# The down projection of a feed-forward stage: seven block products in place of eight, with the sums kept in DRAM

## The chip, the cores and the metric

The kernel runs on one core of a Trainium2 chip. The metric is the device time of one execution in microseconds. The engines are PE (TensorE, matrix products), DVE (VectorE), ACT (ScalarE), POOL (GpSimd) and SP (SyncE, which only issues transfers here). Each engine works through its own list of instructions in order, and instructions of different engines wait for each other by semaphores. PE writes into eight PSUM banks of 128 x 512 float32; the other engines read these.

## The reference, cut to what matters

One transformer block on 512 tokens of width 2048. The change touches its last part alone, the gated feed-forward of width 5632:

```
h = rms_norm(x, pre_ffn_norm)
u = causal_dwconv(h @ w_up, conv_w, conv_b)          # 512 x 11264
gate, up = jnp.split(u, 2, axis=-1)
y = (jax.nn.gelu(gate, approximate=True) * up) @ w_down    # (512 x 5632) @ (5632 x 2048)
x = x + rms_norm(y, post_ffn_norm)
```

## The kernel before, in words

All matrix products are in float32 precision made of two parts: a tile `a` is split into `hi` (rounded by an ACT copy) and `lo = a - hi` (a DVE subtraction; `split`, L132 to L134), and a product is three matmuls, hi·hi + hi·lo + lo·hi. So each weight tile that comes from DRAM costs one ACT and one DVE instruction per 128 x 512 piece before PE can use it.

Work is a list of *units*: a unit is a weight tile of 128 x 1024 (512 KB) and the matmuls that use it. The main loop (L1028 on) runs unit i on PE and, between its matmuls, writes into the program the fetch of unit i+2 and the two halves of the split of unit i+1 (`prepare`), the evacuation of the unit before, and, paced by `tick`, single steps of background work. The order of every engine's list is fixed by this when the program is written; nothing is reordered on the chip.

The feed-forward has 44 column blocks j of 128 (so 88 for gate and up), in 11 groups of four. The up projection of one half of a j is two units of 24 matmuls. The background work of a j (`up_items`) is the convolution's taps (one ACT, two DVE instructions), the polynomial and tanh of the gelu, the gate and the product `prod`, whose result, the activation of 128 x 512 (features x tokens), is split into `gact[j]` = hi, lo. The down projection of group G is written after the first j of group G+1 (`down(G - 1)`): four blocks of 512 output columns g, two units each, 24 matmuls per unit, so 192 matmuls of 512 columns in a row. PE adds over the group in four banks, and `accumulate` (L865 to L870) adds each finished bank to the tile y[t, g] in SBUF by one DVE instruction. The last group is done apart, after the list, from weights kept in `H`.

SBUF has a pool of 37 tiles of 128 x 512 (`slot`), and weights have 3 buffers `raw`, 2 each of `hi` and `lo`, and 4 of `pt`, which serve as a second pair of hi and lo for units with the tag "pt".

Of the kernel before, what the change touches and what calls it, by code (L numbers as in the profile page):

```python
# [34 lines left out]
GROUP = 4  # L35
# [15 lines left out]
def body(ctx, tc, xT, x, gpre, vecs, lam4, tab, onehot, cmpm, wst, wdv, wvs, wvg, w1, w2, wo, wu, wd,  # L51
# [42 lines left out]
    park = dp.tile([PARK, 128, 512], F, name="park")  # L94
    xpark = dp.tile([S, D], F, name="xpark")

    pending = deque()
# [44 lines left out]
    def unit(src, n, mms, prep=None, after=None, start=None):  # L142
        units.append(dict(src=src, n=n, mms=mms, prep=prep, after=after, start=start, late=False, defer=False, tag=None, each=None))

# [669 lines left out]
    conv = {}  # L814
    gact = {}
    y = {}
    ysum = st.tile([128, NT, 4], F, name="ysum")

    def up_items(j, which, b):
# [24 lines left out]
        def prod():  # L844
            c = conv.pop((j, 1))
            V.scalar_tensor_tensor(c, conv.pop((j, 0)), 0.5, c, op0=OP.mult, op1=OP.mult)  # L846
            gact[j] = [slot(R), slot(R)]
            split(gact[j][0], gact[j][1], c)
        return [taps, poly, tanh, gate] if which == 0 else [taps, nothing, nothing, prod]

# [5 lines left out]
    def down_mms(b, hi, lo, G, k, t, first, last):  # L856
        ts = slice(t * 128, (t + 1) * 128)
        for c in range(2):
            gh, gl = gact[G * GROUP + 2 * k + c]
# [12 lines left out]
    NP = GROUP // 2  # L872

    def down(G):
        for g in range(4):
            box = {}
            for k in range(NP):
                def mms(hi, lo, g=g, k=k, box=box):
                    if k == 0:
                        box["b"] = [bank() for _ in range(NT)]  # L880
                    for t in range(NT):
                        down_mms(box["b"][t], hi, lo, G, k, t, k == 0, k == NP - 1)
                        yield
                        if k == NP - 1:
                            accumulate(t, g, box["b"][t], G)
                unit(wd[(G * NP + k) * 4 + g], 1024, mms)

# [77 lines left out]
    raws, his = {}, {}  # L965

    def fetch(i):
        u = units[i]
        r = raws[i] = wp.tile([128, 1024], F, name="raw", tag="raw", bufs=3)
        if i == 0:  # L970
            for c in range(2):
                load_x(c, 1)
                nc.sync.dma_start(r[:, c * 512:(c + 1) * 512], u["src"][:, c * 512:(c + 1) * 512])
            return
        if i < 8:
            load_x(2 * i, 2)
        nc.sync.dma_start(r[:, :u["n"]], u["src"])

    def prepare(i, part):
        u = units[i]  # L980
        n = u["n"]
        if u["prep"]:
            u["prep"](part)
        if part == 0:
            if u["tag"]:
# [5 lines left out]
        o = slice(part * 512, min(n, part * 512 + 512))  # L991
        split(hi[:, o], lo[:, o], raws[i][:, o])
        if part == 1:
            del raws[i]

# [3 lines left out]
    def hold_fetch(m):  # L999
        k, g = divmod(m, 4)  # L1000
        hraw[m] = wp.tile([128, 1024], F, name="raw", tag="raw", bufs=3)
        nc.sync.dma_start(hraw[m], wd[(G * NP + k) * 4 + g])

# [14 lines left out]
    deferred = []  # L1018
    for i in range(N):
        if i + 2 < N:  # L1020
            fetch(i + 2)
# [5 lines left out]
        hi, lo = his.pop(i)  # L1027
        todo = [0, 1] if i + 1 < N else []  # L1028

        def ahead():  # L1030
            if todo:
                prepare(i + 1, todo.pop(0))
            if not todo:
                while deferred:
                    deferred.pop(0)()
        for n, _ in enumerate(u["mms"](hi, lo)):
            if not u["late"]:
                ahead()
            if u["each"]:
                u["each"](n)  # L1040
            tick()
        if u["late"]:
# [27 lines left out]
    def last_sum(t, g):  # L1070
        accumulate(t, g, last[t, g], G)
        j = slot()
# [69 lines left out]
def _layout(i):  # L1142
# [19 lines left out]
    wu = f("w_up").reshape(2, 8, 128, 2, NJ, 128).transpose(4, 3, 0, 2, 1, 5).reshape(NJ * 4, 128, 1024)  # L1162
    wd = f("w_down").reshape(NJ // 2, 2, 128, 4, 512).transpose(0, 3, 2, 1, 4).reshape(NJ * 2, 128, 1024)
    vecs = np.concatenate([col(f("diff_subln")), f("cmp_pos_k").T, f("cmp_pos_v").T,
# [21 lines left out]
```

## Time and profile before

| | us |
|---|---|
| median of 3 runs | 2335.55 (2333.77 to 2335.76) |
| the profiled execution, own time | 2335.62 |
| its span, first to last instruction | 2333.5 |
| PE busy | 2307.7 (99%) |
| DVE busy | 1289.6 (55%) |
| ACT busy | 892.6 (38%) |
| POOL busy | 90.1 (4%) |

Busy is the time with at least one instruction in the engine; what matters is which engine the others wait for. The program moved 276.09 MB by DMA, 118 GB/s on the mean. The trace numbers times from the first instruction; the feed-forward runs from about 900 us to the end.

### The profile page before, as it was taken

The page shows a single profiled execution, that of the slowest core. Times are in us where ns is not written, and L with a number is a line of the kernel's source. Part 1 is how long each engine was busy: PE and PEld are TensorE (multiplying, and loading weights), DVE is VectorE, ACT ScalarE, POOL GpSimd, SP SyncE. Part 2 cuts the span into 40 slices and gives each one's busy share as a digit, 9 for nine tenths or more (in the row PEclk, how much of TensorE's full clock was granted, in tenths as well). Part 3 has the DMA queues.
Part 4 walks back from the last instruction along what each step waited for, and adds up shares of the span by engine and source line. Part 5 has one row for each costly group of instructions (what it writes and reads, how often), then busy time and mean ns, then how long its engine had stood idle before and what let it go on. Part 6 is the DMA issues. An engine that isn't in the chain of part 4 may idle for free.

```text
span 2333.5 us, 28580 instructions
## 1 busy us (share of the span) xinstructions
PE 2307.7 (99%) x10956; PEld 1917.4 (82%) x10956; DVE 1289.6 (55%) x2454; ACT 892.6 (38%) x1823; POOL 90.1 (4%) x145
## 2 busy tenths in 40 slices
PE   9999999999999999999999999999999999999997
PEld 7878888988887779788888888888888888888886
DVE  5366665657786664644545454554545454544557
ACT  6245553444465553423233232323232332323233
POOL 1001100000011101000000000000000000000002
PEclk9999999999999999999999999999999999999999
DMA  8433333432246572222222222222332222323325
GB/s 307 159 97 102 95 96 120 150 115 64 64 163 225 200 244 99 91 100 100 95 97 98 100 95 96 100 100 90 100 100 93 97 99 92 104 94 100 115 94 189
DMA packets 81689, 276.09 MB, mean 118 GB/s; under 512 B 9914, under 2 KB 9914, under 8 KB 81552
## 3 DMA queue, kind: packets, MB, share of 16 engines
q1 hardware_dynamic: 72000, 243.51, 31.6%
q0 software_dynamic: 9552, 30.76, 4.1%
q8 instruction: 86, 1.41, 0.3%
q14 instruction: 51, 0.42, 0.1%
HBM read 260.29 MB, written 17.08 MB: 119 GB/s over the span
## 4 chain that ended last, share of the span: by engine, by line
PE 92%; DVE 3%; DMA 3%; issue 1%; ACT 1%; SPq 0%; POOL 0%; DVEq 0%; ACTq 0%; POOLq 0%
PE b L73 90%; DMA raw<-wo 2%; PE b L353 1%; DVE lo L134 1%; DMA s<-xpark 1%; ACT hi L133 0%; DMA raw<-wdv 0%; DVE s L1090 0%; DMA raw<-wd 0%; DVE H L134 0%; DVE pt L134 0%; PE b L759 0%; DVE H L764 0%; DVE s L752 0%; PE b L457 0%
## 5 line engine op out<-in xcount | busy, mean ns | idle before, releaser
L73 PE MATMUL b<-H,hi 128*128 128x512 f32 (+1 forms) x3776 | 1167.2, 391 | 0.0
L134 DVE TENSOR_TENSOR lo<-raw,hi 128x512 fp32r<-128x512 f32 (+1 forms) x808 | 534.6, 686 | 741.0 <-ACT hi L133 739.9
L133 ACT ACTIVATE hi<-raw 128x512 fp32r<-128x512 f32 (+1 forms) x808 | 472.3, 621 | 895.4 <-PE b L73 747.9
L73 PEld LDWEIGHTS b<-H,hi 128*128 128x128 f32 x3776 | 697.0, 188 | 142.8 <-issue 3.5
L73 PE MATMUL b<-H,lo 128*128 128x512 f32 (+1 forms) x1888 | 733.1, 388 | 0.1
L73 PEld LDWEIGHTS b<-H,lo 128*128 128x128 f32 x1888 | 354.4, 188 | 75.2 <-DVE lo L134 1.6
L73 PE MATMUL b<-hi,s 128*128 128x512 f32 x1280 | 395.6, 389 | 0.0
L73 PE MATMUL b<-hi,H 128*128 128x512 f32 (+2 forms) x1024 | 295.4, 367 | 4.8 <-ACT hi L133 4.8
L73 PEld LDWEIGHTS b<-hi,s 128*128 128x128 f32 x1280 | 240.2, 188 | 49.8
L73 PE MATMUL b<-lo,s 128*128 128x512 f32 x640 | 249.0, 389 | 0.0
L73 PEld LDWEIGHTS b<-hi,H 128*128 128x128 f32 x1024 | 185.2, 188 | 37.7 <-ACT hi L133 8.7
L73 PE MATMUL b<-lo,H 128*128 128x512 f32 (+2 forms) x512 | 188.5, 368 | 4.1 <-DVE lo L134 3.5
L73 PEld LDWEIGHTS b<-lo,s 128*128 128x128 f32 x640 | 120.1, 188 | 25.0
L870 DVE TENSOR_TENSOR s<-s,b 128x512 f32<-128x512 f32 x160 | 107.5, 685 | 43.4 <-PE b L73 41.5
L73 PEld LDWEIGHTS b<-lo,H 128*128 128x128 f32 x512 | 96.3, 188 | 24.3 <-DVE lo L134 10.6
L338 ACT ACTIVATE s<-s,st 128x512 f32<-128x512 f32 (+3 forms) x128 | 71.0, 556 | 105.4 <-DVE st L336 105.4
L133 ACT ACTIVATE s<-s 128x512 fp32r<-128x512 f32 (+1 forms) x72 | 42.0, 583 | 117.4 <-DVE s L846 63.3
L73 PEld LDWEIGHTS b<-pt,s 128*128 128x128 f32 (+1 forms) x480 | 69.3, 166 | 5.7
L73 PE MATMUL b<-pt,s 128*62 128x256 f32 (+3 forms) x480 | 73.5, 302 | 0.0
L336 DVE CUSTOM_DVE_ANT_0 s<-b,bt 128x512 f32<-128x512 f32 (+3 forms) x128 | 57.6, 487 | 27.4 <-PE b L73 27.0
L134 DVE TENSOR_TENSOR s<-s 128x512 fp32r<-128x512 f32 (+1 forms) x72 | 45.5, 632 | 46.8 <-ACT s L133 46.8
L827 DVE SCALAR_TENSOR_TENSOR s<-b,vec,s 128x510 f32<-128x510 f32 x88 | 65.9, 749 | 3.1
(185 smaller groups left out, 1446.1 us busy)
## 6 DMA issues: line engine op xcount, KB each, us to landing
raw<-wu SPq DMA_DIRECT2D x176, 512.0 KB, 3.3
raw<-wd SPq DMA_DIRECT2D x88, 512.0 KB, 3.3
raw<-wst SPq DMA_DIRECT2D x64, 512.0 KB, 3.6
raw<-wo SPq DMA_DIRECT2D x64, 512.0 KB, 3.6
raw<-w SPq DMA_DIRECT2D x16, 512.0 KB, 4.2
raw<-wdv SPq DMA_DIRECT2D x15, 512.0 KB, 7.1
rows_b<-rv POOLq DMA_DIRECT2D x1, 5120.0 KB, 24.8
s<-xT SPq DMA_DIRECT2D x16, 256.0 KB, 6.4
```

The costliest lines, as they stand in the source:

```text
L73: T.matmul(o, a, b, start=start, stop=stop, skip_group_check=True)
L133: A.activation(hi, src, AF.Copy)
L134: V.tensor_tensor(lo, src, hi.bitcast(F), OP.subtract)
L336: V.tensor_tensor_reduce(out=z[:, :n], in0=b[:, :n], in1=bt[:, 384 - 128 * i:384 - 128 * i + n], scale=-1.0, scalar=3e38, op0=OP.add, op1= ...
L338: A.activation(z[:, :n], z[:, :n], AF.Exp, bias=m[:, j:j + 1], scale=-1.0, accum_out=s[:, j:j + 1])
L353: T.transpose(b[:, j * 128:(j + 1) * 128], z[:, j * 128:(j + 1) * 128], ident)
L827: V.scalar_tensor_tensor(c[:, 2:], b[:, :510], w[0], c[:, 2:], op0=OP.mult, op1=OP.add)
L870: V.tensor_tensor(y[t, g], y[t, g], b, OP.add)
```

## The change: what it does

For ten of the eleven groups the product (512 tokens x 512 features) x (512 features x 2048 columns) is cut once in two by two by two blocks: token halves (256), feature halves (two j each), and column halves. With A of blocks 11, 12, 21, 22 (token half, feature half) and weights likewise, eight block products become seven (the Winograd form of Strassen's identity): the left factors are 11, 12, 22 and s1 to s4, sums and differences of blocks of A; the right factors are three plain weight blocks and, for s1, s2, s3 and 22, differences of weight blocks. The function `down(G, q)` writes the seven for one pair q of 512-column blocks; it is called after the first j of the next group (q = 0) and after the second (q = 1).

- A block product is one unit of 12 matmuls of 512 columns (two feature blocks p, two token blocks t of 128, three matmuls each).
- The right factors are made on DVE just before they are split: `less` subtracts two tiles of 128 x 512 (L933), `split` then makes hi on ACT and lo on DVE. This is done per half p.
- The weights of a `q` come as one tile of 512 KB (a) and three as pairs of 256 KB in slots (b, c, d), fetched four units ahead. The main loop may now prepare unit i+2 beside unit i+1; the units have alternating tags (hi/lo and pt).
- The left factors are made in `up_items`: `sums12` and `sums34` are new steps on DVE (four half-width instructions and two splits more per pair of j).
- The products run in three chains of PSUM banks, x, y and z, in the order x y x y x z x. A chain goes on adding in its two banks after each product, and after each product both banks are copied out (ACT, or DVE for one of the two banks of every second product, L967 and L969) into slots, and a POOL DMA writes the slot to one of 16 DRAM tiles `yacc`, or adds it there (`accum_op`, L972).
- `accumulate` is gone; 16 DMAs load y back from DRAM at the last unit (`load_y`).

The diff, cut:

```
-    def tick():
-        pace["ticks"] += 1
-        pace["credit"] += pace["rate"]
+    def tick(weight=1.0):
+        pace["ticks"] += weight
+        pace["credit"] += pace["rate"] * weight
...
+            graw[j] = c
+            if j % 2 == 0:
+                t = slot(R)
+                split(t[:, LH], t[:, RH], c[:, LH])
+                fac[j // 2] = {"11": (t[:, LH], t[:, RH])}
+            else:
+                twin(j // 2, "12", "22", c)
...
+        def sums12():
+            a, b = graw[j - 1], graw[j]
+            c = graw[j, 1] = slot()
+            V.tensor_tensor(c[:, LH], a[:, RH], b[:, RH], OP.add)
+            V.tensor_tensor(c[:, RH], c[:, LH], a[:, LH], OP.subtract)
+            twin(j // 2, "s1", "s2", c)
...
-    def accumulate(t, g, b, G):
-        if G == 0:
-            y[t, g] = slot()
-            V.tensor_copy(y[t, g], b)
-        else:
-            V.tensor_tensor(y[t, g], y[t, g], b, OP.add)
...
+        def less(a, b, dst):
+            def f(p):
+                V.tensor_tensor(at(dst, p), at(a, p), at(b, p), OP.subtract)
+                return at(dst, p)
+            return f
+
+        prods = [("11", "x", (0, 0), plain("a"), [whole("a", 0, 0), halves("b", 0, 1)]),
+                 ("s1", "y", (1, 1), less("b", "a", "a"), [halves("c", 1, 1)]),
+                 ("s2", "x", (0, 1), less("c", "a", "a"), [halves("d", 1, 0)]),
+                 ("s4", "y", (0, 1), plain("c"), []),
+                 ("s3", "x", (1, 1), less("c", "b", "b"), []),
+                 ("12", "z", (0, 0), plain("d"), []),
+                 ("22", "x", (1, 0), less("d", "a", "a"), [])]
...
+            def after(n=n, ch=ch, th=th, ph=ph):
+                for t in range(2):
+                    v = slot()
+                    if t and n % 2:
+                        V.tensor_copy(v, chain[ch][t])
+                    else:
+                        A.activation(v, chain[ch][t], AF.Copy)
+                    key = 2 * th + t, 2 * ph + q
+                    if key in begun:
+                        nc.gpsimd.dma_start(yacc[key], v, accum_op=OP.add)
+                    else:
+                        begun.add(key)
+                        nc.gpsimd.dma_start(yacc[key], v)
+            unit(None, 1024, mms, after=after)
+            units[-1].update(get=lambda gets=gets: [f() for f in gets], raw=raw, defer=True, weight=0.5,
+                             tag="pt" if n % 2 else None)
...
-            if G and j == G * GROUP:
-                down(G - 1)
+            if G and j - G * GROUP < 2:
+                down(G - 1, j - G * GROUP)
+
+    units[-1]["start"] = load_y
...
-        todo = [0, 1] if i + 1 < N else []
+        todo = [(i + 1, part) for part in range(done.get(i + 1, 0), 2)] if i + 1 < N else []
+        if i + 2 < N and units[i + 2]["raw"] and not units[i]["tag"] == units[i + 1]["tag"] == units[i + 2]["tag"]:
+            todo += [(i + 2, part) for part in range(done.get(i + 2, 0), 2)]
```

How the lists stand now. First ACT, in the middle of the feed-forward, q = 0 of a group. `hi_` and `pt_` tiles are hi parts of right factors, `raw_` and other `s_` inputs are weights, `b_` are PSUM banks; L830 is the taps, L134 a hi copy, L969 a bank copied out (b_13515 and b_13516 are chain x, b_13541 is chain y).

```order
1090 L134 ACTIVATE pt_13501<-raw_13334 128x512 x2
1091 L134 ACTIVATE hi_13520<-raw_13334 128x512 x2
1092 L830 ACTIVATE s_13534<-b_13436,vec_75 128x512
1093 L134 ACTIVATE pt_13546<-s_13377 128x512
1094 L134 ACTIVATE pt_13546<-s_13378 128x512
1095 L969 ACTIVATE s_13555<-b_13515 128x512
1096 L969 ACTIVATE s_13558<-b_13516 128x512
1097 L134 ACTIVATE hi_13570<-s_13336 128x512
1098 L134 ACTIVATE hi_13570<-s_13337 128x512
1099 L969 ACTIVATE s_13581<-b_13541 128x512
```

The copies out of a bank are new on ACT, and each stands behind the hi copies of the products after next: bank x of product 11 (1095) behind the hi copies of s2 (1091) and s4 (1093, 1094), bank y of s1 (1099) behind those of s3 (1097, 1098).

The same place on DVE: L933 is a difference of weights, L135 a lo part, L831 and L832 the taps.

```order
1772 L933 TENSOR_TENSOR raw_13334<-s_13336,raw_13334 128x512
1773 L135 TENSOR_TENSOR pt_13502<-raw_13334,pt_13501 128x512
1774 L933 TENSOR_TENSOR raw_13334<-s_13337,raw_13334 128x512
1775 L135 TENSOR_TENSOR pt_13502<-raw_13334,pt_13501 128x512
1776 L933 TENSOR_TENSOR raw_13334<-s_13377,raw_13334 128x512
1777 L135 TENSOR_TENSOR lo_13521<-raw_13334,hi_13520 128x512
1778 L933 TENSOR_TENSOR raw_13334<-s_13378,raw_13334 128x512
1779 L135 TENSOR_TENSOR lo_13521<-raw_13334,hi_13520 128x512
1780 L831 SCALAR_TENSOR_TENSOR s_13534<-b_13436,vec_75,s_13534 128x511
1781 L832 SCALAR_TENSOR_TENSOR s_13534<-b_13436,vec_75,s_13534 128x510
1782 L135 TENSOR_TENSOR pt_13547<-s_13377,pt_13546 128x512
1783 L135 TENSOR_TENSOR pt_13547<-s_13378,pt_13546 128x512
```

Every difference is followed at once by the lo part of the same half, which needs ACT's hi copy in between. Before, DVE's list at the start of a down projection held lo parts, taps and the sums of L870, and no differences:

```order
1722 L134 TENSOR_TENSOR lo_13848<-raw_13802,hi_13847 128x512 x2
1723 L826 SCALAR_TENSOR_TENSOR s_13859<-b_13762,vec_75,s_13859 128x511
1724 L827 SCALAR_TENSOR_TENSOR s_13859<-b_13762,vec_75,s_13859 128x510
1725 L134 TENSOR_TENSOR lo_13884<-raw_13835,hi_13883 128x512
1726 L846 SCALAR_TENSOR_TENSOR s_13859<-s_13781,s_13859 128x512
1727 L134 TENSOR_TENSOR s_13889<-s_13859,s_13888 128x512
1728 L870 TENSOR_TENSOR s_9456<-s_9456,b_13837 128x512
1729 L134 TENSOR_TENSOR lo_13884<-raw_13835,hi_13883 128x512
1730 L870 TENSOR_TENSOR s_9466<-s_9466,b_13838 128x512
```

Second, ACT in q = 1 of the same group, around the copies of chain x after s2 (1134, 1135), for which the matmuls of s3 wait:

```order
1130 L134 ACTIVATE s_13932<-s_13878 128x512
1131 L134 ACTIVATE s_13945<-s_13942 128x512
1132 L134 ACTIVATE pt_13952<-s_13776 128x512
1133 L134 ACTIVATE pt_13952<-s_13777 128x512
1134 L969 ACTIVATE s_13961<-b_13859 128x512
1135 L969 ACTIVATE s_13964<-b_13860 128x512
1136 L134 ACTIVATE s_13970<-s_13967 128x512
1137 L134 ACTIVATE hi_13983<-raw_13695 128x512 x2
```

Here the hi parts of the activation (1130) and of s1 and s2 (1131, from `sums12`) have come ahead of the copies; in q = 0 one half-width hi part stands at this place.

## Rows read from the trace of the kernel before

**Rows 1.** The page: busy time by engine.
```profile
PE 2307.7 (99%) x10956; PEld 1917.4 (82%) x10956; DVE 1289.6 (55%) x2454; ACT 892.6 (38%) x1823; POOL 90.1 (4%) x145
```
**Rows 2.** The page: the chain that ended last, shares by engine.
```profile
PE 92%; DVE 3%; DMA 3%; issue 1%; ACT 1%; SPq 0%; POOL 0%; DVEq 0%; ACTq 0%; POOLq 0%
```
**Rows 3.** Stretches: length; busy us of PE, PEld, DVE, ACT, POOL; PE clock; DMA.
```profile
1300.00:1430.55 130.55, 130.55 (x578) 108.10 (x577) 64.89 (x101) 40.17 (x68) 0.00 (x0) 1.00 0.29 97
1515.48:1559.00 43.52, 43.52 (x193) 36.04 (x192) 22.89 (x35) 10.51 (x18) 0.00 (x0) 1.00 0.29 99
```
**Rows 4.** Groups from 1515.48 to 1559.00 us: count, busy us, mean ns, idle before.
```profile
L73 PE MATMUL b<-hi,s 128*128 128x512 f32 x128 | 39.5, 389 | 0.0
L73 PE MATMUL b<-lo,s 128*128 128x512 f32 x64 | 24.9, 389 | 0.0
```
**Rows 5.** Timeline of PE, the first matmul of that stretch: start, us, what.
```profile
1515.48 0.39 PE L73 MATMUL b<-hi,s 128*128 128x512 f32 x1
```
**Rows 6.** Timeline of DVE around that start.
```profile
1509.25 0.69 DVE L834 TENSOR_TENSOR s<-s 128x512 f32<-128x512 f32 x1
...
1512.37 0.69 DVE L134 TENSOR_TENSOR lo<-raw,hi 128x512 fp32r<-128x512 f32 x1
1516.12 1.29 DVE L134 TENSOR_TENSOR lo<-raw,hi 128x512 fp32r<-128x512 f32 x2 [3.07 <-ACT hi L133]
1517.33 0.74 DVE L826 SCALAR_TENSOR_TENSOR s<-b,vec,s 128x511 f32<-128x511 f32 x1
1518.11 0.75 DVE L827 SCALAR_TENSOR_TENSOR s<-b,vec,s 128x510 f32<-128x510 f32 x1
```
**Rows 7.** Timeline of ACT around that start.
```profile
1509.97 0.63 ACT L838 ACTIVATE s<-s 128x512 f32<-128x512 f32 x1 [1.22 <-DVE s L834]
...
1515.46 1.15 ACT L133 ACTIVATE hi<-raw 128x512 fp32r<-128x512 f32 x2 [3.81 <-PE b L73]
1516.52 0.77 ACT L825 ACTIVATE s<-b,vec 128x512 f32<-128x512 f32 x1
```
**Rows 8.** Groups by form, whole span: count, busy us, mean ns of one.
```profile
L868 DVE COPY s<-b 128x512 f32<-128x512 f32 x16 | 10.9, 689 | 4.2 <-PE b L73 4.0
L134 DVE TENSOR_TENSOR pt<-b,pt 128x256 fp32r<-128x256 f32 x24 | 9.4, 418 | 1.9 <-ACT pt L133 1.9
L133 ACT ACTIVATE pt<-b 128x256 fp32r<-128x256 f32 x24 | 8.2, 377 | 5.8 <-PE b L353 5.7
L485 ACT ACTIVATE s<-b 128x512 f32<-128x512 f32 x8 | 4.8, 598 | 9.3 <-PE b L73 9.3
```
**Rows 9.** Timeline around a wait of PE for ACT.
```profile
858.31 1.15 ACT L133 ACTIVATE hi<-raw 128x512 fp32r<-128x512 f32 x2 [2.68 <-DMA raw<-wo]
...
858.99 0.49 PE L73 MATMUL b<-hi,H 128*128 128x512 f32 x1 [0.82 <-ACT hi L133]
```
**Rows 10.** Timeline of DVE beside eight DMA issues of POOL.
```profile
807.82 4.32 POOL L753 DMA_DIRECT2D xpark<-s  x8
...
809.59 0.75 DVE L752 SCALAR_TENSOR_TENSOR s<-s,st 128x512 f32<-128x512 f32 x1
```
**Rows 11.** DMA: POOL's queue (packets, MB, share); its stores, us to landing.
```profile
q0 software_dynamic: 9552, 30.76, 4.1%
...
xpark<-s POOLq DMA_DIRECT2D x16, 256.0 KB, 5.3
```
**Rows 12.** Timeline of PE, its longest wait after the first 20 us.
```profile
722.39 0.50 PE L73 MATMUL b<-hi,H 128*128 128x512 f32 x1 [1.11 <-ACT hi L133]
```
**Rows 13.** Stretches at the end; columns as in rows 3.
```profile
2318.00:2321.00 3.00, 2.76 (x13) 1.95 (x11) 2.58 (x3) 0.72 (x1) 1.39 (x2) 1.00 0.29 110
2321.00:2323.00 2.00, 0.00 (x0) 0.00 (x0) 2.00 (x4) 0.93 (x3) 0.23 (x1) 1.00 0.97 363
2323.00:2325.00 2.00, 0.00 (x0) 0.00 (x0) 2.00 (x4) 1.66 (x6) 1.04 (x1) 0.69 0.85 225
```
**Rows 14.** Timeline of ACT in the tail: the last weights of the last group.
```profile
2288.50 1.15 ACT L133 ACTIVATE H<-raw 128x512 fp32r<-128x512 f32 x2 [2.99 <-DMA raw<-wd]
```

More of the change, by code (lines that the diff above doesn't have):

```diff
@@ L95, in body @@
     xpark = dp.tile([S, D], F, name="xpark")
+    yacc = {(t, g): dp.tile([128, 512], F, name="yacc%d%d" % (t, g)) for t in range(NT) for g in range(4)}
     pending = deque()
@@ L142, in unit @@
     def unit(src, n, mms, prep=None, after=None, start=None):
-        units.append(dict(src=src, n=n, mms=mms, prep=prep, after=after, start=start, late=False, defer=False, tag=None, each=None))
+        units.append(dict(src=src, n=n, mms=mms, prep=prep, after=after, start=start, late=False, defer=False, tag=None, each=None,
+                          get=None, raw=None, weight=1.0))
     def stationary(srcs, evac, start=None):
@@ new lines, in wd_at, with down, whole, f @@
+    def wd_at(G, q, r, c):
+        return wd[((G * 2 + q) * 2 + r) * 2 + c]
+    def down(G, q):
+        t_ = {}
+        def whole(name, r, c):
+            def f():
+                t_[name] = wp.tile([128, 1024], F, name="raw", tag="raw", bufs=3)
+                nc.sync.dma_start(t_[name], wd_at(G, q, r, c))
+            return f
+        def halves(name, r, c):
+            def f():
+                t_[name] = [slot(), slot()]
+                for p in range(2):
+                    nc.sync.dma_start(t_[name][p], wd_at(G, q, r, c)[:, p * 512:(p + 1) * 512])
+            return f
+        def at(name, p):
+            v = t_[name]
+            return v[p] if isinstance(v, list) else v[:, p * 512:(p + 1) * 512]
+        def plain(name):
+            return lambda p: at(name, p)
+        def less(a, b, dst):
+            def f(p):
+                V.tensor_tensor(at(dst, p), at(a, p), at(b, p), OP.subtract)
+                return at(dst, p)
+            return f
+        prods = [("11", "x", (0, 0), plain("a"), [whole("a", 0, 0), halves("b", 0, 1)]),
[5 more added lines that the diff above has]
+                 ("22", "x", (1, 0), less("d", "a", "a"), [])]
+        chain = {}
+        count = {}
+        for n, (left, ch, (th, ph), raw, gets) in enumerate(prods):
+            def mms(hi, lo, left=left, ch=ch):
+                if ch not in chain:
+                    chain[ch] = [bank(), bank()]
+                first = count.get(ch, 0) == 0
+                count[ch] = 1
+                for p in range(2):
+                    fh, fl = fac[2 * G + p][left]
+                    w = slice(p * 512, (p + 1) * 512)
+                    for t in range(2):
+                        b = chain[ch][t]
+                        ts = slice(t * 128, (t + 1) * 128)
+                        mm(b, fh[:, ts], hi[:, w], first and p == 0, False)
+                        mm(b, fh[:, ts], lo[:, w], False, False)
+                        mm(b, fl[:, ts], hi[:, w], False, p == 1)
+                        yield
+            def after(n=n, ch=ch, th=th, ph=ph):
+                for t in range(2):
+                    v = slot()
[12 more added lines that the diff above has]
+                             tag="pt" if n % 2 else None)
@@ L888, in body, with load_y @@
+    begun = set()
+    def load_y():
+        for t in range(NT):
+            for g in range(4):
+                y[t, g] = slot()
+                nc.gpsimd.dma_start(y[t, g], yacc[t, g])
     NG = NJ // GROUP
@@ L983, in prepare @@
             u["prep"](part)
+        done[i] = part + 1
         if part == 0:
@@ L991, in prepare @@
         o = slice(part * 512, min(n, part * 512 + 512))
-        split(hi[:, o], lo[:, o], raws[i][:, o])
+        split(hi[:, o], lo[:, o], u["raw"](part) if u["raw"] else raws[i][:, o])
         if part == 1:
-            del raws[i]
+            raws.pop(i, None)
     G = NG - 1
@@ L1019, in body @@
     for i in range(N):
+        if i + 4 < N and units[i + 4]["get"]:
+            units[i + 4]["get"]()
         if i + 2 < N:
@@ L1070, in last_sum @@
     def last_sum(t, g):
-        accumulate(t, g, last[t, g], G)
+        V.tensor_tensor(y[t, g], y[t, g], last[t, g], OP.add)
         j = slot()
```

49 lines of the change are left out of this document (29 added, 20 removed).

## The prediction, made before the change was run

> **What bounds the kernel now.** I read the page first: PE is busy for 99% of the span [rows 1], and the chain that ended last runs through PE for 92% of it [rows 2]. So a matmul less is time won, as long as nothing else takes PE's place. Next I read the stretches. In a whole group of the feed-forward (130.55 us) PE never pauses, DVE works 64.89 us and ACT 40.17 us; in a down projection (43.52 us) it is 22.89 and 10.51 us [rows 3]. That stretch holds 128 + 64 = 192 matmuls [rows 4], so one starts every 43.52 / 192 = 0.2267 us, though its own row says 0.39 us: they overlap. On the mean there is much room on DVE and ACT. The mean decides nothing, though: what counts is which instruction PE waits for in the ten stretches that change, and so I follow DVE's and ACT's lists there, by the order shown above.
>
> **What is removed.** 192 matmuls per group become 14 products of 12, which is 168. Ten groups lose 240 matmuls: 240 x 0.2267 = 54.4 us. The sums in SBUF (L870, 160 DVE instructions less the 16 that stay) and DVE's copies of the first group lay beside PE and win nothing.
>
> **What is added: unit prices.** A DVE instruction on 128 x 512 with two inputs takes 0.69 us, and the next starts 0.60 us after it (two take 1.29) [rows 6]. An ACT copy takes 0.62 us, the next starts 0.53 us after it (two take 1.15) [rows 7]. From DVE to ACT the handover takes 1509.97 - (1509.25 + 0.69) = 0.03 us, from ACT to DVE 1516.12 - (1515.46 + 0.62) = 0.04 us [rows 6, 7]. I use 0.04 for both. The taps cost ACT 0.77 us and DVE two steps of 0.78 us (1517.33 to 1518.11) [rows 6, 7]. A bank copied out takes 0.60 us on ACT (I let the next start after 0.53) and 0.69 us on DVE; half-width split parts take 0.38 us on ACT and 0.42 us on DVE [rows 8]. PE starts 858.99 - (858.31 + 0.62) = 0.06 us after ACT releases it, and its first matmul then takes 0.1 us more than the usual 0.39 [rows 9]; I charge 0.1.
>
> **The step that decides.** Half a block of a weight difference needs the difference on DVE, hi on ACT, lo on DVE, and DVE's list has the next difference only behind that lo. So each half occupies DVE's list for 0.69 + 0.04 + 0.62 + 0.04 + 0.60 = 1.99 us, of which DVE idles 0.7. A block is two halves, 4.0 us, while PE uses a block up in 12 x 0.2267 = 2.72 us. Four of the seven blocks of a q are differences. DVE can run ahead, but only by what the program's order allows, and the copies of the banks stand on ACT's list behind the hi copies of these blocks. Since chain x is added to again one product later, PE must wait for the copy.
>
> I follow q = 0 with time 0 at PE's first product matmul (1515.48 in the old trace). The lists up to there are the old ones, so DVE starts its second lo at 1512.37 - 1515.48 = -3.1 [rows 5, 6] and is free for s1's first difference at -2.5.
> - s1, two halves: differences at -2.5 and -0.5, lo parts done at 1.6; s2: differences at 1.5 and 3.5, last hi at 4.2 to 4.8, last lo from 4.9. DVE is free at 5.5.
> - ACT after that hi: taps 4.7 to 5.5, two hi copies for s4, then the banks of product 11: first out at 7.1, second at 7.6. The matmuls of s2, due at 2 x 2.72 = 5.4, start at 7.2: **wait 1.7**.
> - DVE: taps until 7.05, two lo parts until 8.25, s3's halves: differences at 8.25 and 10.25, last hi 11.0 to 11.6, then its lo and the copy of s1's second bank (12.25 to 12.95). ACT: first bank of s1 out at 12.1. s4, due at 7.2 + 2.7 = 9.9, starts at 12.2, and its fourth matmul waits 0.1 for DVE's copy: **wait 2.4**.
> - DVE: `prod` 12.9 to 13.6; hi (half width) until 14.0; ACT two hi copies until 15.05, banks of s2 out at 15.6. s3, due at 15.0, starts at 15.6: **wait 0.6**.
> - Product 22: differences at 15.7 and 17.7, last hi until 19.1, banks of s3 out at 20.1 and 20.6. Product 22 is due at 15.6 + 5.4 = 21.0: no wait. The phase ends at 23.8 where 84 matmuls alone need 19.0: **4.7 us lost**.
>
> q = 1 is the same until DVE's copy at 12.95. Then more lies ahead of s2's banks on ACT: hi of `prod` is full width (13.6 to 14.2), DVE makes its lo and the two half-width sums of `sums12` (to 15.7), ACT their hi (15.75 to 16.4) and two more; the bank is out at 17.95. s3, due at 15.0, starts at 18.0: **wait 3.0**. DVE then has lo of those, two halves of `sums34`, its split, and only at 20.35 the first difference of 22; last hi until 23.7, then on ACT one bank of s4 and s3's, out at 24.75. Product 22, due at 23.45, starts at 24.8: **wait 1.35**. With the first two waits (1.7, 2.4), **8.45 us lost**.
>
> So a group loses 13.2 us and wins 5.44. Ten groups: +132 - 54.4 = +77.6 us. DVE's and ACT's lists are clear again within the 22 us of up projection that follow each q, so nothing is carried on.
>
> **What else is added.** The 280 stores and accumulating DMAs of 256 KB (73.4 MB) are put on POOL's list, which is empty here. The trace has no accumulating DMA. From below: a plain store; POOL's queue moved 30.76 MB in 4.1% of 2333.5 us, 321 GB/s [rows 11], so 0.82 us of all engines each, 23 us per group beside weights that leave 71% of the DMA time free (share 0.29) [rows 3]. From above: read, read and write, three times that, 69 us of the 0.71 x 125 = 89 us free. Both fit. POOL must wait for s2's DMA to land before it issues s4's on the same tile, about 4 us later, against a landing of 5.3 us [rows 11]; that holds POOL for a microsecond or so, and by the built program's waits a slot so held is needed again some 15 to 20 us later at the soonest. I take 0. POOL's issues do not hold up DVE either: beside eight of them (0.54 us each) a DVE instruction took 0.75 us [rows 10] as elsewhere. The Trainium skill ("SBUF — State Buffer", Who interferes with whom) says that DVE in its two-port modes and GpSimd's descriptor writing block each other; the trace shows nothing of it in the two-input instructions that make up the path here, and by that rule up to 28 x 0.54 = 15 us a group would come on top.
>
> In the tail 16 loads of y (4.2 MB, 13 us at 321 GB/s) come beside the last weights, which ACT already waits 2.99 us for [rows 14]; PE has slack of about 5 us there (the last weights, split by 2290.5, are used from the 85th of 192 matmuls that end at 2320.8). Between 0 and 13 - 5 = 8 us; I take 1, since y is needed late.
>
> The profiled execution took 2335.62 us, 0.07 above the median shown, so: 2335.6 + 77.6 + 1 = **2414 us**, slower by 3.4%.
>
> **Rivals.**
> 1. *The waits are hidden, and it is faster.* For it speak the fetches four units ahead, the units prepared two ahead, and the means: DVE would work about 83 of 125 us a group. It decides when a group waits under 5.44 us, which needs the 51 us of DVE and ACT steps of both q to be some 15% shorter than summed; with no wait left it is 2335.6 - 54.4 = 2281 us. Against it: every price above is a row, and the order is fixed. 9%; between, within 0.2% (4.7 us, about what this kernel's measurement can tell from no change), 3%.
> 2. *The clock falls in the waits.* The granted clock was 1.00 after a wait of 1.11 us [rows 12]. After the last matmul (ended 2320.76) it held 1.00 to 2323 and had 0.69 on the mean from 2323 to 2325, so 2.4 GHz became 1.2 GHz about 3.0 us after the end [rows 13]. My longest wait is 3.0 us, in the middle of others. One product at 1.2 GHz costs 2.7 us more, one or two per group, part of it swallowed by the next wait: +10 to +50, 2425 to 2465 us. The Trainium skill ("TensorE: Matmul & The Clock Gate", HAM oscillation) tells of kernels whose idle gaps between bursts of matmuls bring the half clock back; by that rule this rival would be the likeliest. 18%.
> 3. *Accumulating DMAs are far slower than three transfers.* If one holds all engines for over 89 / 28 = 3.2 us, four times a plain store, they set the pace; at six times, a group takes 28 x 4.9 + 0.29 x 130.55 = 175 us, +45 a group, 2790 us. Or each lands after more than 15 us and slots run out. 10%.
>
> **The numbers.** My forecast (the waits on DVE and ACT, clock full) has 60%; its own range is 2375 to 2450, waits of 9.3 to 16.8 us a group: a step's error of 10% on 51 us is 5 us a group downward less what PE's slack absorbs, and upward unseen semaphore waits. The clock rival extends it to 2465, and I add a little for a mild form of the third: **2370 to 2475**. Faster 9%, same 3%, slower 88%.
>
> **What would show it.** Right: PE's waits at the matmuls of down are ended by ACT L969, 1.7 and 2.4 us at s2 and s4 in both q, 3.0 us at s3 of q = 1; DVE L933 and L135 alternate with idle 0.7 us ended by ACT L134; the feed-forward's period is 125.1 + 13 = 138 us instead of 130.55; the up projections stay without waits. Wrong: PE's waits ended by DMA or POOL, a clock under 1.00 in the feed-forward, or a period near 125 us.

## The result and the profile after

| | us |
|---|---|
| kernel before, median | 2335.12 |
| changed kernel, median of 4 runs | 2461.36 (2459.84 to 2462.69) |
| ratio, 95% interval | 1.0541 (1.0523 to 1.0559) |
| forecast | 2414, range 2370 to 2475 |

Slower by 5.4%. The sign, the engine that PE waits for and the price of a step came as forecast; the loss is 126 us where 79 were forecast. The profiled execution took 2459.84 us, its span is 2458.0.

The page of the changed kernel, busy time by engine, answers to [rows 1]; under it the queue of POOL and the landing times answer to [rows 11].

```profile
PE 2317.9 (94%) x10716; PEld 1896.9 (77%) x10716; DVE 1450.8 (59%) x2754; ACT 1090.0 (44%) x2203; POOL 341.2 (14%) x441
...
q0 software_dynamic: 50128, 108.37, 22.7%
...
raw<-wu SPq DMA_DIRECT2D x176, 512.0 KB, 4.3
yacc<-s POOLq DMA_DIRECT2D x280, 256.0 KB, 7.6
```

PE has 240 matmuls fewer and is busy 10 us longer: some of them ran at the lower clock. Its waits from 1100 to 2300 us (which instruction waited for which; us in total, times, longest):

```profile
PE b L73 <- ACT s L969: 92.4, 48, 4.1
```

So nearly every wait of PE is for a bank copied out by ACT, as the forecast said. Stretches of one group, with the columns of [rows 3]: the whole period, q = 0, q = 1, the up projection between them, and a piece of q = 0.

```profile
1300.00:1442.55 142.55, 131.06 (x549) 105.35 (x548) 80.11 (x129) 58.90 (x105) 24.60 (x28) 0.96 0.59 140
1569.72:1595.58 25.86, 21.70 (x86) 16.38 (x84) 17.96 (x29) 13.63 (x25) 7.26 (x10) 0.93 0.54 88
1617.34:1647.33 29.99, 23.26 (x85) 17.51 (x84) 21.10 (x35) 15.10 (x27) 8.68 (x11) 0.89 0.48 73
1595.58:1617.34 21.76, 21.76 (x98) 18.02 (x96) 8.63 (x14) 7.41 (x13) 5.12 (x6) 1.00 1.01 258
1579.90:1583.30 3.40, 3.40 (x9) 2.17 (x7) 1.97 (x4) 1.27 (x3) 0.89 (x1) 0.50 0.92 130
```

The period is 142.6 us where 138.3 were forecast and 130.55 were before. The up projection has no wait (21.76 us is 96 matmuls), so all of the loss lies in q = 0 (25.9 us, forecast 23.8) and q = 1 (30.0, forecast 27.5). The last row says that PE ran at 1.2 GHz for a while in the middle. PE's waits of over 0.2 us in these two stretches, from its timeline (start of the matmul that waited, its length, the wait in brackets):

```profile
1578.79 0.50 PE L73 MATMUL b<-hi,s 128*128 128x512 f32 x1 [3.47 <-ACT s L969]
1583.83 3.19 PE L73 MATMUL b<-pt,s 128*128 128x512 f32 x12 [0.46 <-ACT s L969]
1587.24 0.50 PE L73 MATMUL b<-hi,s 128*128 128x512 f32 x1 [0.23 <-ACT s L969]
...
1626.56 0.50 PE L73 MATMUL b<-hi,s 128*128 128x512 f32 x1 [3.62 <-ACT s L969]
1631.61 3.17 PE L73 MATMUL b<-pt,s 128*128 128x512 f32 x12 [0.48 <-ACT s L969]
1637.41 0.50 PE L73 MATMUL b<-hi,s 128*128 128x512 f32 x1 [2.63 <-ACT s L969]
```

The waits stand where the forecast put them, ahead of s2, s4 and s3, but the first of each q is 3.5 us and not 1.7. Those ahead of s4 are 0.5 us where 2.4 were forecast, because s2 ran at the lower clock (the row of 0.50) and used that time up. (The profile counts a wait from the end of the matmul before, 0.39 - 0.23 = 0.16 us after the next one was due; the forecast counted from when it was due, so 0.16 has to be added to compare.) Two views say why the first wait is so long. First DVE's list ahead of q = 0 (PE's first product matmul is at 1569.72):

```profile
1557.24 0.42 DVE L873 TENSOR_TENSOR s<-s 128x256 f32<-128x256 f32 x1
1557.69 0.42 DVE L874 TENSOR_TENSOR s<-s 128x256 f32<-128x256 f32 x1
1558.81 0.69 DVE L135 TENSOR_TENSOR s<-s 128x512 fp32r<-128x512 f32 x1 [0.70 <-ACT s L134]
1559.42 0.42 DVE L880 TENSOR_TENSOR s<-s 128x256 f32<-128x256 f32 x1
1559.76 0.42 DVE L881 TENSOR_TENSOR s<-s 128x256 f32<-128x256 f32 x1
1560.87 0.69 DVE L135 TENSOR_TENSOR s<-s 128x512 fp32r<-128x512 f32 x1 [0.70 <-ACT s L134]
...
1569.16 0.69 DVE L933 TENSOR_TENSOR raw<-s,raw 128x512 f32<-128x512 f32 x1
1570.54 0.69 DVE L135 TENSOR_TENSOR pt<-raw,pt 128x512 fp32r<-128x512 f32 x1 [0.70 <-ACT pt L134]
1571.15 0.69 DVE L933 TENSOR_TENSOR raw<-s,raw 128x512 f32<-128x512 f32 x1
```

The differences follow each other at 1.99 us with 0.70 us idle for ACT, to the hundredth what was forecast. But the first starts at 1569.16, 0.56 us ahead of PE, where 2.5 were forecast. Ahead of it stand the new factor sums (L873 to L881) of the pair of j just finished and their two round trips to ACT.

Second, ahead of q = 1, ACT waits for weights of the up projection, and SP, which issues them, had issued nothing for 28 us:

```profile
1601.99 1.15 ACT L134 ACTIVATE hi<-raw 128x512 fp32r<-128x512 f32 x2 [4.09 <-DMA raw<-wu]
1608.60 1.15 ACT L134 ACTIVATE hi<-raw 128x512 fp32r<-128x512 f32 x2 [5.45 <-DMA raw<-wu]
```

```profile
1562.80 0.33 SPq L1082 DMA_DIRECT2D raw<-wu  x1
1591.59 0.33 SPq L914 DMA_DIRECT2D raw<-wd  x1
1592.01 0.86 SPq L921 DMA_DIRECT2D s<-wd  x2
1594.17 0.33 SPq L1082 DMA_DIRECT2D raw<-wu  x1
```

The waits of SP's queue from 1100 to 2300 us name what it waited for:

```profile
SPq L914 <- DVE lo L135: 257.7, 17, 28.5
```

L914 is the load of block a of q = 1 into a `raw` buffer; it waits for the last lo part of product 22 of q = 0, which still uses the buffer of the old block a. The up projection's next load stands behind it in SP's list and takes the buffer that comes free after that (1594.17). The loads that now go out together meet full DMA engines. From 1590 to 1612 us POOL's queue (q0) and SP's (q1) took, as a share of the 16 engines (last column), and a load of the up projection took to landing (last column, us):

```profile
q0 software_dynamic: 1168, 2.13, 58.5%
q1 hardware_dynamic: 1370, 3.46, 46.5%
...
raw<-wu SPq DMA_DIRECT2D x4, 512.0 KB, 9.2
```

Over the whole run such a load landed after 4.3 us.

### The profile page after: what moved, and what is told of

Same layout as the page of the kernel before. It is cut to its first block, busy times and chain, and to the rows that moved or that the text cites. A ratio compares the mean times of both kernels' runs of the same rounds, so it can differ in the third digit from the quotient of the medians.

```text
span 2458.0 us, 29731 instructions
## 1 busy us (share of the span) xinstructions
PE 2317.9 (94%) x10716; PEld 1896.9 (77%) x10716; DVE 1450.8 (59%) x2754; ACT 1090.0 (44%) x2203; POOL 341.2 (14%) x441
## 3 DMA queue, kind: packets, MB, share of 16 engines
q0 software_dynamic: 50128, 108.37, 22.7%
## 5 line engine op out<-in xcount | busy, mean ns | idle before, releaser
L135 DVE TENSOR_TENSOR lo<-raw,hi 128x512 fp32r<-128x512 f32 (+1 forms) x768 | 508.1, 686 | 666.2 <-ACT hi L134 664.3
L134 ACT ACTIVATE hi<-raw 128x512 fp32r<-128x512 f32 (+1 forms) x768 | 451.7, 622 | 644.0 <-PE b L73 368.8
L972 POOL DMA_DIRECT2D yacc<-s x264 | 233.3, 1263 | 1069.6 <-ACT s L969 1020.6
L73 PE MATMUL b<-hi,s 128*128 128x512 f32 x640 | 244.7, 447 | 97.5 <-ACT s L969 97.5
L73 PE MATMUL b<-pt,s 128*128 128x512 f32 (+4 forms) x1200 | 255.7, 362 | 12.2 <-ACT s L969 11.9
L73 PEld LDWEIGHTS b<-pt,s 128*128 128x128 f32 (+1 forms) x1200 | 204.4, 182 | 60.9 <-ACT s L969 22.2
L73 PEld LDWEIGHTS b<-hi,s 128*128 128x128 f32 x640 | 138.4, 216 | 145.6 <-ACT s L969 114.4
L73 PE MATMUL b<-lo,s 128*128 128x512 f32 x320 | 140.8, 440 | 0.0
L134 ACT ACTIVATE s<-s 128x512 fp32r<-128x512 f32 (+2 forms) x112 | 62.9, 562 | 172.7 <-DVE s L851 65.6
L969 ACT ACTIVATE s<-b 128x512 f32<-128x512 f32 x220 | 118.9, 588 | 0.0
L73 PEld LDWEIGHTS b<-lo,H 128*128 128x128 f32 x512 | 96.3, 188 | 24.4 <-DVE lo L135 10.6
L135 DVE TENSOR_TENSOR s<-s 128x512 fp32r<-128x512 f32 (+2 forms) x112 | 67.8, 606 | 70.4 <-ACT s L134 70.4
L933 DVE TENSOR_TENSOR raw<-s,raw 128x512 f32<-128x512 f32 x120 | 82.1, 684 | 0.0
```

The costliest lines, as they stand in the source:

```text
L73: T.matmul(o, a, b, start=start, stop=stop, skip_group_check=True)
L134: A.activation(hi, src, AF.Copy)
L135: V.tensor_tensor(lo, src, hi.bitcast(F), OP.subtract)
L933: V.tensor_tensor(at(dst, p), at(a, p), at(b, p), OP.subtract)
L969: A.activation(v, chain[ch][t], AF.Copy)
L972: nc.gpsimd.dma_start(yacc[key], v, accum_op=OP.add)
```

## The experiments

Theory 1: PE waits for the lists of DVE and ACT (round trips of differences, bank copies behind them, and what starts those lists late). Theory 2: the accumulating DMAs hold loads and slots up. Theory 3: the clock that falls in the waits is a large part of the miss. The lengths of q = 0 and q = 1 below are medians over the groups, read from PE's timeline from the first product matmul to the end of the last (84 matmuls alone: 84 x 0.2267 + 0.16 = 19.2 us).

| run | us | ratio to before (interval) | q = 0 | q = 1 |
|---|---|---|---|---|
| changed kernel | 2461.36 | 1.0541 (1.0523 to 1.0559) | 26.0 | 29.9 |
| e1_both_halves | 2357.44 | 1.0088 (1.0070 to 1.0106) | 21.8 | 23.8 |
| e2_copies_first | 2517.33 | 1.0777 (1.0761 to 1.0793) | 26.3 | 33.1 |
| e3_both | 2381.98 | 1.0199 (1.0181 to 1.0217) | 20.8 | 27.0 |
| e4_plain_stores | 2452.07 | 1.0499 (1.0483 to 1.0514) | 26.0 | 28.7 |
| e5_no_sums | 2407.33 | 1.0305 (1.0287 to 1.0323) | 24.2 | 26.5 |
| e6_fillers | 2460.26 | 1.0531 (1.0515 to 1.0547) | 26.9 | 29.0 |
| e7_halves_and_later_sums | 2319.94 | 0.9930 (0.9915 to 0.9945) | 21.8 | 20.4 |
| e9_spread | 2292.92 | 0.9815 (0.9801 to 0.9830) | spread | spread |
| e11_a_in_slots | 2439.32 | 1.0443 (1.0427 to 1.0459) | 26.0 | 27.7 |
| e12_spread_alone | 2302.12 | 0.9856 (0.9840 to 0.9873) | spread | spread |
| e13_no_sums_a_in_slots | 2389.36 | 1.0227 (1.0212 to 1.0242) | 25.0 | 24.2 |

**e1_both_halves.** Both halves of a difference ahead of the first split:

```
+    made = {}
...
-        split(hi[:, o], lo[:, o], u["raw"](part) if u["raw"] else raws[i][:, o])
+        if u["raw"] and part == 0:
+            made[i] = [u["raw"](p) for p in range(2)]
+        split(hi[:, o], lo[:, o], made[i][part] if u["raw"] else raws[i][:, o])
```

> A difference block's two subtractions are both made at its first half, ahead of that half's hi and lo pieces; the arithmetic is unchanged. Theory 1 (the lists): a difference block occupies DVE for 0.69 + 0.69 + 0.60 + 0.60 = 2.6 us instead of 4.0, since DVE's second subtraction no longer stands behind the round trip to ACT; s1, s2, s3 and 22 then lose about 1.4 us less each. The first wait stays, because the late start of the chain and the bank copies are as before. Of the 17.6 us that a group loses in the changed kernel some 9 go: about 2355 to 2375 us, still slower than before. Theory 2 (the accumulating DMAs give buffers back late, or hold the loads up): within 10 us of 2461. [...]

104 us of the 126 are gone by a new order of four instructions per difference block, no work less. In q = 0 the waits are now

```profile
1540.37 0.50 PE L73 MATMUL b<-hi,s 128*128 128x512 f32 x1 [0.63 <-ACT s L969]
1543.97 3.24 PE L73 MATMUL b<-pt,s 128*128 128x512 f32 x12 [0.59 <-ACT s L969]
1547.44 0.50 PE L73 MATMUL b<-hi,s 128*128 128x512 f32 x1 [0.23 <-ACT s L969]
```

and in q = 1 one is left, ahead of s3:

```profile
1591.20 0.50 PE L73 MATMUL b<-hi,s 128*128 128x512 f32 x1 [2.65 <-ACT s L969]
```

This is theory 1; neither DMA nor slots were touched. The time is in the expected range, but that the first wait would stay was wrong: it fell from 3.47 to 0.63 us. With the waits most of the half clock went too (the mean clock is 0.991, in the changed kernel 0.978), so this run alone does not separate theory 3 from theory 1; e6_fillers does.

**e2_copies_first, e3_both.** The copies out of the banks ahead of the next splits, alone and with e1's edit:

```
+    copies = []
...
         def ahead():
+            while copies:
+                copies.pop(0)()
             if todo:
                 prepare(*todo.pop(0))
...
-        while todo or deferred:
+        while todo or deferred or copies:
...
-                deferred.append(u["after"])
+                (copies if u["raw"] else deferred).append(u["after"])
```

> The copies of a finished chain out of its banks are written ahead of the next block's splits in the lists of ACT and DVE instead of behind them; nothing else changes. Theory 1: s2's hi pieces are not waited for behind the copies any more than now, but the banks that s2, s4 and s3 write into come free sooner: the first wait of a down stretch falls from 3.6 to about 1 us, DVE's chain of 4.0 us per difference block still sets the end; a group loses about 12 instead of 17.6, 2400 to 2415 us. If the waits ahead of s2 and s3 are for the split pieces and not for the banks, the change is within 10 us of 2461. Theory 2 (slots held by the accumulating DMAs): no change.

> Both edits together: both subtractions first, and the copies out of the banks ahead of the splits. Theory 1: the first down stretch of a group loses about 1 us, the second about 3 to 4 (its start is late by a weight load): 2305 to 2335 us, at or below the kernel before. Theory 2 (DMAs) and theory 3 (clock) alone: over 2400 us.

Both missed: 56 and 25 us slower than without the edit. The wait ahead of s2 did fall, to 2.45 us in q = 0 (from 3.47), but the DVE copy of s1's bank (1606.03) now stands ahead of s3's differences (from 1606.63), and the wait comes back ahead of s3:

```profile
1603.84 0.50 PE L73 MATMUL b<-hi,s 128*128 128x512 f32 x1 [2.45 <-ACT s L969]
1612.35 0.69 PE L73 MATMUL b<-hi,s 128*128 128x512 f32 x1 [2.77 <-ACT s L969]
```

So q = 0 of e2_copies_first is no shorter than in the changed kernel (in e3_both it is 1 us shorter than in e1_both_halves). The loss lies elsewhere: q = 1 is 3 us longer in both runs, and in e2_copies_first 1 to 4 us more a group go in the up projection behind q = 0. Neither was followed; the cause is open. That ACT's copy ends PE's wait does not mean that it stands too late in the list.

**e4_plain_stores.** `nc.gpsimd.dma_start(yacc[key], v, accum_op=OP.add)` without its `accum_op`.

> The stores into yacc are made without accumulating, so that its sums are missing from the output (each store overwrites the one before); the number and size of the stores are the same. It measures what accumulating costs. Theory 1: the waits of the lists stay; only the late weight loads ahead of the second down stretch go, about 2 us per group: 2435 to 2455 us. Theory 2 (the accumulating DMAs are the cause): most of the 124 us go, under 2380 us. If accumulating is hidden altogether: within 5 us of 2461.

9.3 us of the 126, nearly all in q = 1, where the up projection's loads land sooner: from 1587.8 to 1609.8 us of this run, which answers to the stretch above, POOL's queue took 24.4% of the engines and such a load landed after 6.5 us. So theory 2 has a small part in the loss and is not the main cause. The page has for the queue, for POOL's issues of the stores (count, busy us, mean ns) and for their landing:

```profile
q0 software_dynamic: 33232, 108.37, 12.1%
...
L972 POOL DMA_DIRECT2D yacc<-s x264 | 141.7, 540 | 1146.8 <-ACT s L969 1119.1
...
yacc<-s POOLq DMA_DIRECT2D x280, 256.0 KB, 4.7
```

**e5_no_sums.**

```
-        return [taps, nothing, nothing, prod] + ([sums12, sums34] if j % 2 and j < NJ - GROUP else [])
+        return [taps, nothing, nothing, prod] + []
...
-                    fh, fl = fac[2 * G + p][left]
+                    fh, fl = fac[2 * G + p][{"s1": "11", "s2": "12", "s3": "22", "s4": "12"}.get(left, left)]
```

> The factor sums of the activations (sums12, sums34 and their splits) are left out, and s1 to s4 use the plain factors in their place, so the output is another; all blocks, differences, copies and stores stay. It measures what the new factor steps cost, for which the prediction had nothing. Theory 1 (they stand in the lists of DVE and ACT just ahead of the first down stretch and inside the second): the first wait of q=0 falls from 3.5 to about 1.7 us as predicted, the wait of 2.6 us ahead of s3 in q=1 goes, 5 to 6.5 us per group, 2395 to 2410 us, about the forecast. If the late start has another cause, only the wait ahead of s3 can go: 2425 to 2440. If neither: within 5 us of 2461.

54 us of the 126. The waits in a q = 0, which starts at 1405.57, are 1.52 and 2.01 us (forecast 1.7 and 2.4), and DVE's first difference there starts 2.52 us ahead of PE (forecast 2.5):

```profile
1412.68 0.50 PE L73 MATMUL b<-hi,s 128*128 128x512 f32 x1 [1.52 <-ACT s L969]
1417.73 3.18 PE L73 MATMUL b<-pt,s 128*128 128x512 f32 x12 [2.01 <-ACT s L969]
```

```profile
1403.05 0.69 DVE L933 TENSOR_TENSOR raw<-s,raw 128x512 f32<-128x512 f32 x1
```

**e6_fillers.** Matmuls into a spare bank behind s1 and s4:

```
-            def mms(hi, lo, left=left, ch=ch):
+            def mms(hi, lo, left=left, ch=ch, n=n):
...
+                        if p and t and n in ((1, 3) if q else (1,)):
+                            d = bank()
+                            for _ in range(8 if n == 1 else 6):
+                                mm(d, fh[:, ts], hi[:, w], True, True)
```

> PE is given matmuls into a spare bank that nobody reads: 8 behind s1 in both down stretches, and 6 behind s4 in the second, 1.8 and 1.4 us inside waits of 3.5 and 2.6 us, so that the clock need not fall. Adds work, leaves nothing out. Theory 1 (the lists set the end; a slow s2 is swallowed by the wait ahead of s4): only the slow s3 of q=1 is won, up to 2 us per group, 2438 to 2455 us. Theory 3 (the clock is a large part of the miss): the half-clock stretches go and most of the 45 us that they cost: under 2425 us. If the clock falls in spite of the fillers: 2455 to 2470.

The stretch from 1100 to 2280 us of the changed kernel and of this one (columns as in [rows 3]):

```profile
1100.00:2280.00 1180.00, 1092.83 (x4585) 881.53 (x4584) 668.66 (x1074) 493.57 (x872) 197.88 (x224) 0.96 0.59 140
```

```profile
1100.00:2280.00 1180.00, 1115.30 (x4765) 902.84 (x4765) 669.56 (x1075) 494.56 (x873) 197.51 (x224) 0.98 0.58 140
```

The mean clocks of 0.96 and 0.98 stand for 85 and 41 us at 1.2 GHz, by the trace's clock records. The time is the same within 1.1 us: theory 1's 2438 to 2455 was missed, and the last case came true, since the clock fell in spite of the fillers in six q = 0 of ten. Two q = 0 of this run, at full clock and with such a stretch:

```profile
1425.48:1451.30 25.82, 21.92 (x93) 16.96 (x92) 17.96 (x29) 13.63 (x25) 7.72 (x10) 1.00 0.55 91
1567.09:1593.80 26.71, 23.02 (x93) 18.21 (x92) 17.96 (x29) 13.63 (x25) 7.70 (x11) 0.94 0.57 101
```

The first is as long as the changed kernel's q = 0 at a clock of 0.93 (25.86 us). There the slow product is s2, and the wait ahead of s4 gave back what it lost: 0.5 us against 2.0 here. In the second row the slow product is s4, the wait behind it is short (0.2 us in the first), and 0.9 us is lost. In q = 1 the stretch from s2 on is 0.2 us shorter than in the changed kernel. So the clock cost the changed kernel nothing in eight q = 0 of ten, 0.9 us in the other two and some 0.2 us in a q = 1, about 4 us of the 126: theory 3 falls as a main cause of the miss.

**e7_halves_and_later_sums.** e1's edit, and the sums of a group's first pair nine turns later:

```
-        return [taps, nothing, nothing, prod] + ([sums12, sums34] if j % 2 and j < NJ - GROUP else [])
+        return [taps, nothing, nothing, prod] + (([nothing] * 9 if j % GROUP == 1 else []) + [sums12, sums34] if j % 2 and j < NJ - GROUP else [])
```

> Both subtractions first (as in e1_both_halves), and the factor sums of a group's first pair are made nine turns later, behind the second down stretch instead of inside it. Theory 1: the wait of 2.65 us ahead of s3 in q=1, and the half clock behind it, go: 2.7 to 4 us per group from 2357, so 2318 to 2332 us, below the kernel before. If that wait is for something else (bank copies, weight loads): within 8 us of 2357.

As theory 1 has it, and faster than the kernel before: the sums inside q = 1 were what held s3's bank copies back. PE's waits from 1100 to 2300 us are a fifth of the changed kernel's 92.4:

```profile
PE b L73 <- ACT s L969: 17.2, 36, 0.6
```

**e9_spread, e12_spread_alone.** The fourteen products between the eight up units of two j; with e1's edit, and without.

```
-        prods = [("11", "x", (0, 0), plain("a"), [whole("a", 0, 0), halves("b", 0, 1)]),
+        prods = [("11", "x", (0, 0), plain("a"), [halves("a", 0, 0), halves("b", 0, 1)]),
...
-                             tag="pt" if n % 2 else None)
+                             tag="pt")
...
-            if G and j - G * GROUP < 2:
-                down(G - 1, j - G * GROUP)
+            if G and j - G * GROUP == 1:
+                ups = units[-8:]
...
+                for k, n in enumerate((0, 2, 2, 2, 3, 2, 2, 1)):
+                    units.append(ups.pop(0))
+                    units.extend(dn[:n])
+                    del dn[:n]
```

> Both subtractions first, and the 14 blocks of a group's down stretches are spread between the eight up blocks of the same two j in the order up up 11 s1 up s2 s4 up s3 12 up 22 11 s1 up s2 s4 up s3 12 up 22; block 00 of wd is loaded in halves into slots like the others. Theory 1: an up block gives the lists of DVE and ACT 5.44 us for one plain block, so the differences, the copies and the factor sums find room, PE waits nowhere for long, and the saved matmuls show: 2335 - 54 = 2281 us and some waits, 2281 to 2305. Theory 2 (the accumulating DMAs hold slots and loads up): waits remain, over 2330.

> The order of e9_spread without e1's edit: the subtractions are each made ahead of their half again, so a difference block holds DVE's list for 4.0 us, but an up block's 5.44 us lies between every one or two of them. Theory 1 in its plain form (it is the run of four difference blocks in seven that PE waits for): at most a microsecond per group is lost, 2290 to 2305 us. If the round trip of a single block is already too long: 2310 to 2340.

Both inside what theory 1 gave. e9_spread is the fastest kernel of this study, 1.85% below the one before. One group of it, and PE's waits from 1100 to 2300 us:

```profile
1498.60:1624.30 125.70, 125.43 (x553) 103.53 (x553) 80.19 (x131) 59.41 (x106) 24.50 (x28) 1.00 0.68 159
```

```profile
PE b L73 <- DVE lo L135: 2.4, 9, 0.3
```

With the same 80 us of DVE work a group as the changed kernel, and the same accumulating DMAs, PE waits 0.27 us a group, and the clock stays at 2.4 GHz. Ten periods are 10 x (130.55 - 125.70) = 48.5 us shorter, 43 of which show in the time. Some 4 of the rest are lost from 780 to 970 us, ahead of the first changed stretch, where PE is busy for 180.6 us against 184.4 before; it is so in some runs and not in others (e7_halves_and_later_sums has 184.2), and why is open.

**e11_a_in_slots, e13_no_sums_a_in_slots.** Block a of `wd` in halves into slots (the first edit of e9_spread), alone and with e5's.

> Only block 00 of wd is loaded otherwise: in two halves into slots, as the other three blocks are, instead of whole into one of the three raw buffers; everything else is the changed kernel. Theory 1a (q=1 starts late because the raw buffer that block 00 holds until 22 has been split is the one that the next up block's load waits for): the first wait of q=1 falls from 3.6 to about 1.7 us, q=0 is as before, 1.5 to 3 us per group, 2430 to 2446 us. Theory 2 (the loads are late because the accumulating DMAs crowd them): within 5 us of 2461.

> The factor sums left out (as in e5_no_sums, the output is another for it) and block 00 in slots (as in e11_a_in_slots), so that both down stretches start as the prediction took it, with nothing of the lists carried over. Theory 1: the first wait is about 1.5 us in both, no wait of 2.6 us ahead of s3, about 5 us lost in q=0 and 5 to 5.5 in q=1: 2380 to 2395 us, what the lists alone cost. If q=1 still starts late: 2400 to 2410.

22 us alone, 18 on top of e5. In e11_a_in_slots q = 1 loses what the forecast said, 27.7 us in length against 27.5 + 0.16 (the last matmul's overlap); its waits, in a stretch that starts at 1893.27:

```profile
1900.34 0.50 PE L73 MATMUL b<-hi,s 128*128 128x512 f32 x1 [1.46 <-ACT s L969]
1905.38 4.57 PE L73 MATMUL b<-pt,s 128*128 128x512 f32 x12 [2.03 <-ACT s L969]
1911.19 0.51 PE L73 MATMUL b<-hi,s 128*128 128x512 f32 x1 [1.24 <-ACT s L969]
1917.95 0.50 PE L73 MATMUL b<-hi,s 128*128 128x512 f32 x1 [1.00 <-ACT s L969]
```

The forecast had 1.7, 2.4, 3.0 and 1.35, against these with 0.16 added to each; the slow matmuls of s4 (12 in 4.57 us) took 1.7 us out of the third. So it is the raw buffer that starts q = 1 late: without it ACT waits for no load there. The accumulating DMAs lengthen the delay, since the late loads meet them (e4_plain_stores: 1.2 of these 2.2 us a group); the two gains overlap and can't be added. In e13_no_sums_a_in_slots both q are alike, 24 to 25 us, and 2389.36 - 2335.88 + 54.4 = 108 us are left, 5.4 us per q: what round trips and copies cost with both out, the half clock included (10 of the 20 q have a stretch of it and are 1.0 us longer, 25.1 against 24.1).

## Why the prediction came out as it did

- **The range: held partly by luck.** For its own mechanism the prediction gave 2375 to 2450, and 2461 lies outside. It is inside 2370 to 2475 because that was widened for a falling clock and for slow accumulating DMAs, while most of the miss comes from two terms of its own mechanism that it had at nothing (below).
- **The saved matmuls, 54.4 us: right.** In e9_spread, with the waits gone, a period lost 4.85 of the 5.44 us.
- **The step that decides, 1.99 us per half and 4.0 per difference block: right**, and shown twice: the row, and e1_both_halves, which takes the second round trip out and wins 104 us.
- **The waits that follow: right in place and cause**, and in size wherever the lists start as assumed: 1.52 and 2.01 us in q = 0 without the sums (1.68 and 2.17 as the forecast counted, for 1.7 and 2.4), 27.7 us for q = 1 without the late load. With both out, a q loses 5.4 us on the mean where 4.7 were summed for a q = 0.
- **Wrong: "The lists up to there are the old ones".** They are not: the change's own `sums12` and `sums34` of the last pair stand in the up projection just ahead of q = 0, with two round trips more, and delay the first difference from -2.5 to -0.56 us. The forecast followed them in q = 1, where it saw them, and costed them at nothing ahead of q = 0. q = 0 is 26.0 us instead of 23.8 + 0.16: 2.0 us a group, 20 us.
- **Wrong: "nothing is carried on".** The forecast counted POOL's queue and not SP's. Block a holds one of three raw buffers from its load to the last lo of product 22; the next a, fetched four units ahead, waits for it at the head of SP's list, and the up projection's weights behind it. It also took the room on the DMA engines from a mean share of 0.29; in the up projection behind q = 0 the share was 1.01. q = 1 is 29.9 us instead of 27.5 + 0.16: 2.2 us a group, 22 us, and e11_a_in_slots wins 22. With these two terms the sum is 2414 + 20 + 22 = 2456, against 2461 measured; some 4 of the rest were lost from 780 to 970 us (PE busy 180.1 us, 184.4 before), as in e9_spread.
- **Accumulating DMAs taken at 0: nearly.** Accumulating costs 9.3 us (e4_plain_stores), nearly all of it in q = 1; no run leaves the stores out. POOL's queue took 0.227 x 2458.0 = 558 us of all engines against 0.041 x 2333.5 = 96 before; less 13 for the loads of y, that is 1.6 us for each of the 280, twice a plain store of [rows 11] and inside the bounds.
- **The tail's 1 us: right in size.** From the last product to the end there are 100.7 us with two j of up projection (43.5 us), before 121.5 with three (65.3): 57.1 against 56.3.
- **Rival 1 (hidden): wrong for this order, right for another.** The room on DVE and ACT was there on the mean; e12_spread_alone shows that their lists need only an up unit between every one to three products.
- **Rival 2 (the clock): it happened and cost little here.** A clock under 1.00 in the feed-forward was one of the prediction's signs of being wrong. The clock fell to 1.2 GHz in the products behind the long waits, 85 us from 1100 to 2280 us. The rule of the Trainium skill on this ("TensorE: Matmul & The Clock Gate", HAM oscillation), that idle gaps between bursts bring the half clock back, agrees with the row of 0.50. But the slow product of most q = 0 was s2, and the next wait ends when ACT's list says so: about 4 us were lost by the clock (e6_fillers). Where the wait behind the slow product is short, it does cost: 1.6 us in q = 1 of e1_both_halves, 23.8 us with a stretch of it and 22.2 without.
- **The other rule cited ("SBUF — State Buffer", Who interferes with whom)**, by which DVE in its two-port modes and POOL's descriptor writing would block each other: no row here shows it. POOL issued 24.6 us a group, and the differences that ran beside its issues took 0.68 us as the others did. The same section of the Trainium skill says that `tensor_tensor`, the instruction of the differences, has no two-port mode, so the prediction's 15 us a group did not follow from it.

## What to carry to other kernels

Where a tight stretch of one engine is fed by a chain across two in-order lists, price the chain by its round trips, then ask where the lists stand when the stretch begins: every new instruction ahead of it counts, and so does each queue that loads what the lists work on, with the buffers that its head waits for. Issuing the independent half of a pair ahead of the other's round trip cost nothing and gave back 104 of 126 us. Where the means say there is room, spread the stretch among units that are light on the same lists, before counting saved matmuls as lost.

## What the runs showed of the hardware that was not expected

- A DMA that accumulates into DRAM held its queue's engines longer: 22.7% of 2458.0 us against 12.1% of 2453.0 for the same bytes stored plainly, 261 us of all engines for 264 DMAs of 256 KB, or 0.99 us more each. It landed after 7.6 instead of 4.7 us, and POOL's 264 issues were busy for 233.3 instead of 141.7 us, 0.88 instead of 0.54 us each.
- The granted clock was 0.50 in products behind waits of 3.5 and 2.6 us in the middle of dense matmuls, but not behind each: in e1_both_halves the same 2.6 us ahead of s3 was followed by it in seven q = 1 of nine and not in two. It stayed 1.00 from 1100 us on where no wait was over 0.6 us (e7_halves_and_later_sums).
